# Weight sums of a decoder layer in four steps, each set behind a finished piece of the scan

## The chip, the cores and the metric

The kernel runs on 1 core of one Trainium2 chip. The metric is the device time of one execution in microseconds. The kernel before ran at a median of 1055.19 us over 3 runs (1046.66 to 1056.02). The engines are named as the profile names them: PE (TensorE, matrix products; PEld is its weight load), DVE (VectorE), ACT (ScalarE), POOL (GpSimd) and SP (SyncE, which only issues DMAs here).

## What is computed

One decoder layer in float32 over 16 learned leading tokens and 512 tokens of width 1024, with a token mixer of two branches and an MLP:

```python
u = rmsnorm(h, mix_norm_w[i])
proj = u @ w_in[i]
...
y_pool = pool_mixer(u_pool, pool_w_group[i], pool_scale[i]) @ w_pool_up[i]
y_ssd = mamba2_branch(z, xbc, dt_raw, conv_w[i], conv_b[i], dt_bias[i], a_log[i],
                      d_skip[i], ssd_norm_w[i]) @ w_ssd_out[i]
h = h + (gate_pool * y_pool + gate_ssd * y_ssd) @ w_o[i]

v = rmsnorm(h, mlp_norm_w[i])
hid = jax.nn.relu(v @ w_ff1[i])
h = h + (hid * hid) @ w_ff2[i]
```

The pool mixer subtracts each channel from its causal mean over 2, 4, 8 or 16 tokens and mixes groups of 256 channels. The Mamba-2 branch has 8 groups of 4 heads; each group projects x, B, C and z, runs a short causal convolution over x, B and C, and scans the tokens in chunks of 128 with decays that come from dt.

## The kernel before

Channels lie on the 128 partitions and tokens along the free axis. Every float32 product is made from a high and a low part of each operand (`whi`/`wlo` for weights, `uh`/`ul` for the normed input), three matmuls for one product. Weights arrive from `in_w` in blocks of 128 x 1024 through three `raw` buffers: SP issues the load, ACT rounds the block to `whi` (L94), DVE forms the rest as `wlo` (L96).

Some products are done in pairs with seven half-size products instead of eight (a Strassen-Winograd scheme). They need sums of weight quarters: t1 = b11 + b12, s3 = b12 + b22, t2 = t1 + b22 and t4 = t2 + b21. These are formed in DRAM by accumulating DMAs that POOL issues, one **set** after the other (`weight_sums`, L807). There are 16 sets: 3 for the scan's projections (`fx`, used from group 4 on), 6 for the first MLP matrix (`f1`) and 7 for the second (`f2`, which need t1 and s3 alone). The profile calls their results `fx_t`, `fx_s`, `f_t` and `f_s`. Seven sets are issued in groups 0 to 6, three in the pool stage, six ahead of the MLP.

The stages in order of time are: the projection of group 0 (`group_proj`, L498) with norm and dt; four gates and the normed input (`norm_u`, whose `u_d` goes to DRAM); then for each group g the scan (`ssd`, L558) woven with the projection of group g + 1; then the pool stage (`pool_pair`, L930, and `pool_mix`); the merge with gates; w_o; and the MLP.

- `weave` (L687) takes turns: one piece of the scan, then one piece of the list `fill`. The list is worked through one generator after the other: the next group's projection first, then `sums_of_u` (sums of u halves, loaded back from `u_d`), then `weight_sums_at`.
- `ssd` has seven pieces: decay exponentials; states and mask (L638); two halves of y (L646 to L659); squares and their rounded sum `qh` (L663 to L666); the norm factor; the normed output. It begins with the load of `abc`, the decay rows of the group's heads to all partitions (L566), into a single buffer that the `py` products (L652) of the group before read last. ACT uses it at L597.
- `tc.issue_after(i)` makes an engine issue the instructions of a block behind instruction i of that engine. Apart from this and the data dependences, the order on each engine comes from a planner that simulates the program with modelled times and takes what is ready, earlier program text first. On the chip each engine follows that order strictly. POOL waits in front of a DMA for everything that the DMA needs, so what stands behind it in the queue waits too.
- In the groups a set is placed behind the `abc` load (or the last u load) of the same group, L823 to L830.
- POOL's queue also carries the stores of `acs_d` (L373), `u_d` (L403), gates (`gate_d`, L709) and output parts (`acc_d`, L743 and L774), the loads of u halves (L840), of `acc` and of the gates `m1` for the merge (L1003 and L1005), and `ht` (L1146).
- In `pool_pair` seven products run per pair, A11, A12, S2, S1, S3, S4 and A22. A12 has a one-bank PSUM tile `y`. The others go into two halves of one two-bank tile: `c` (A11, S2, S3, A22) and `z` (S1, S4). L964 to L977 read them between the products.

Of the kernel before, what the change touches and what calls it, by code (L numbers as in the profile page):

```python
# [50 lines left out]
BC_PAIRS = (5, 6)  # L51
PAIRS = [(k, g) for g in range(G) for k in "bx" if g in (BC_PAIRS if k == "b" else X_PAIRS)]

SETS_AT = {0: 1, 1: 1, 2: 1, 3: 1, 4: 1, 5: 1, 6: 1}
SETS_POOL = 3

PLAIN = 4
# [6 lines left out]
def kernel(ctx: ExitStack, tc, xT, x, w, fx, f1, f2, vec, fnw, out):  # L64
# [88 lines left out]
    dec = const.tile([P, 4, HEADS], F32, name="dec")  # L153
    cdec = const.tile([P, 4, HEADS], F32, name="cdec")
    wmeta = const.tile([P, HEADS], F32, name="wmeta")
    dve.memset(wmeta, 0.0)

    u_stack = ExitStack()
# [246 lines left out]
            dve.tensor_tensor(ul[k], xt[k], uh[k].bitcast(F32), op=ALU.subtract)  # L405


    def conv(dst, src, ct):
        n = dst.shape[-1]
        e = src.shape[-1] - n  # L410
        act.activation(dst, src[:, e:], AF.Identity, bias=col(V_CB, ct), scale=col(V_CW, ct * 4 + 3))
        for j in range(1, 4):
            o = max(0, j - e)
            dve.scalar_tensor_tensor(dst[:, o:], src[:, e + o - j : e + n - j],
                                     col(V_CW, ct * 4 + 3 - j), dst[:, o:], op0=ALU.mult, op1=ALU.add)
        act.activation(dst, dst, AF.Silu)

    def group_tiles(g):
        xc = gc.tile([P, 2, L], F32, tag="xc", name=f"xc{g}")
# [78 lines left out]
    def group_proj(g, cur, gate=None):  # L498

        first = g == 0  # L500
        xc, bt, ct, zt = cur

        def plain(dst, t, skip):
            if first and (dst is bt or dst is ct):
                view = viewB if dst is bt else viewC
            else:
                runs, view = wide(psum2(f"px{g}_{t}"), skip)
                proj(runs, block(), X if first else U)
            conv(dst, first_raw(t, view, skip) if first else view, t)
# [36 lines left out]
        if first:  # L546
            dve.tensor_tensor(zt, ps.rearrange("p (i t) -> p i t", i=2),
                              rsb[:, NM:].unsqueeze(1).to_broadcast([P, 2, SEQ]), op=ALU.mult)
            act.activation(zf, zf, AF.Silu)
        else:  # L550
            act.activation(zf, ps, AF.Silu)
        yield
# [5 lines left out]
    def ssd(g, cur):  # L558
# [52 lines left out]

        if g < G - 1:
            done[g] = decay()
        yield

        pc = psum1(f"pcb{g}")
# [19 lines left out]
        for rs_ in ((slice(0, 2), slice(2, R)) if g == G - 1 else (slice(0, R),)):  # L636
            n = rs_.stop - rs_.start
            masked[g] = dve.tensor_tensor(dm[:, rs_], dm[:, rs_], cbm.unsqueeze(1).to_broadcast([P, n, 4, P]),  # L638
                                          op=ALU.mult)
        yield  # L640

        yt = gs.tile([P, 2, SEQ], F32, tag="yt", name=f"yt{g}")
        for i in range(2):
            po = psum1(f"po{g}_{i}")
            for c in range(4):
                pe.matmul(po[:, c * P : (c + 1) * P],  # L646
                          flat(st[c])[:, i * P : (i + 1) * P], ct[:, ctok(c)], start=True, stop=True)
            py = psum1(f"py{g}_{i}")
            for c in range(4):
                for j in range(2):  # L650
                    r = 2 * i + j
                    pe.matmul(py[64 * j : 64 * j + 64, c * P : (c + 1) * P],  # L652
                              xdt[:, c, r, :], dm[:, r, c, :], start=True, stop=True)
            y = yt[:, i, :]
            dve.tensor_tensor(y, po, eb[:, i, :], op=ALU.mult)
            dve.tensor_tensor(y, y, py, op=ALU.add)
            dve.scalar_tensor_tensor(y, xc[:, i, NM:], col(V_DS, 2 * g + i), y,
                                     op0=ALU.mult, op1=ALU.add)
            dve.tensor_tensor(y, y, zt[:, i, :], op=ALU.mult)  # L659
            yield  # L660
# [3 lines left out]
        dve.tensor_tensor(sq[:, 0, :], sq[:, 0, :], sq[:, 1, :], op=ALU.add)  # L664
        qh, ql = col_sums(f"g{g}", sq[:, 0, :], gs, ("qh", "ql"))
        yield  # L666
        pn = psum1(f"png{g}")
        pe.matmul(pn, ones_r, qh, start=True, stop=False)
# [40 lines left out]
            nc.gpsimd.dma_start(gate_d[d], o)  # L709


    cur = group_tiles(0)
# [33 lines left out]
    def out_part():  # L746
# [42 lines left out]
        for d in range(2, NK):  # L789
# [5 lines left out]

    sets = [("fx", n) for n in range(fx.shape[0])] + [
            ("f2", 0), ("f2", 1), ("f1", 0), ("f1", 1), ("f1", 2), ("f2", 2), ("f2", 3), ("f1", 3),
            ("f2", 4), ("f1", 4), ("f2", 5), ("f1", 5), ("f2", 6)]  # L800
    assert len(sets) == fx.shape[0] + f1.shape[0] + f2.shape[0]
    SUMS = {"fx": ("t1", "s3", "t2", "t4"), "f1": ("t1", "s3", "t2", "t4"), "f2": ("t1", "s3")}
    wsum = {(*t, n): dram.tile([P, 1040], F32, name="{}{}_{}".format(*t, n))[:, :1024]
            for t in sets for n in SUMS[t[0]]}
    sums_load = {}

    def weight_sums():  # L807
        t = sets.pop(0)
        src = {"fx": fx, "f1": f1, "f2": f2}[t[0]][t[1]]
        o = {n: wsum[(*t, n)] for n in SUMS[t[0]]}  # L810
        put = nc.gpsimd.dma_start
        put(o["t1"], src[B11])
        put(o["s3"], src[B12])
        put(o["t1"], src[B12], accum_op=ALU.add)
        end = put(o["s3"], src[B22], accum_op=ALU.add)
        if "t2" in o:
            put(o["t2"], o["t1"])
            put(o["t2"], src[B22], accum_op=ALU.add)
            put(o["t4"], o["t2"])
            end = put(o["t4"], src[B21], accum_op=ALU.add)  # L820
        return end

    def weight_sums_at(g):  # L823

        with tc.issue_after(sums_load.get(g, abc_load[g]).ins):
            end = weight_sums()
        for _ in range(SETS_AT[g] - 1):
            with tc.issue_after(end.ins):
                end = weight_sums()
        yield  # L830

    def sums_of_u(ks, g):

        one, two = HF
# [1 line left out]
        def load(k):  # L836
            a, b = raw_pair("u", k)
            with tc.issue_after(abc_load[g].ins):
                for t, kk in ((a, k), (b, k + 4)):
                    sums_load[g] = nc.gpsimd.dma_start(t, u_d[kk])  # L840
            return a, b

        def combine(a, b, behind):
# [86 lines left out]
    def pool_pair(p, behind=None):  # L930
# [92 lines left out]
    for n in range(1, 4):  # L1023
# [765 lines left out]
```

## Time and profile before

| What | us |
| --- | --- |
| runs, median of 3 | 1055.19 (1046.66 to 1056.02) |
| the profiled execution, its own time | 1056.63 |
| its span, first to last instruction | 1054.9 |
| ACT busy | 617.6 |
| DVE busy | 805.7 |
| POOL busy, issue of DMAs among it | 111.0 |

The mean granted clock of PE in that execution was 0.978. A row of the order in time reads: start in us, length in us, engine, line, operation, output<-inputs, shapes, count, and in brackets how long the engine was idle before it and what ended that. A row of the chain that ended last has start, length and what the chain spent that time in. A row of the DMA list has output<-input, issuing queue, count, KB of one, and the median us from issue to landing. SP's and POOL's DMA rows show the issue, not the transfer.

### The profile page before, as it was taken

Reading aid. Unit: us, or ns where it says so; the run is one execution under the profiler, and the core shown is the slowest. Engines: PE = TensorE matmul, PEld = TensorE weight load, DVE = VectorE, ACT = ScalarE, POOL = GpSimd, SP = SyncE. Lnnn points to the kernel's source line nnn. Section 1 sums busy time; section 2 is a strip of 40 time slices with the busy share of each in tenths; the row PEclk is TensorE's granted clock in tenths of the full one; section 3 lists DMA queues with packets and bytes.
Section 4 is the critical chain, followed back from the end, with each engine's and each line's share of the span. In section 5 each row is a group of like instructions: output and inputs, shape, how many; then the busy total and the mean of one; then the engine's idle time right before and its main releaser. Section 6 shows DMA issues by size and latency. Waiting matters only on the chain.

```text
span 1054.9 us, 15609 instructions
## 1 busy us (share of the span) xinstructions
PE 1012.0 (96%) x6023; PEld 886.6 (84%) x6023; DVE 805.7 (76%) x1163; ACT 617.6 (59%) x873; POOL 111.0 (11%) x178
## 2 busy tenths in 40 slices
PE   9999799999899899999998999999999999999997
PEld 7889698988687788988987888888889999999986
DVE  7978588968743667989577765787898788788785
ACT  7666749485925534866433443348755666665654
POOL 0131110121001100101321000121111000000000
PEclk9999899999899799999999999999999999999999
DMA  7376583587256734764878653369898745544532
GB/s 251 99 284 170 175 219 111 186 195 248 65 196 193 206 109 152 168 181 111 225 235 244 185 209 100 136 166 275 263 272 240 223 141 160 180 144 157 159 100 80
DMA packets 62922, 190.28 MB, mean 180 GB/s; under 512 B 7360, under 2 KB 8704, under 8 KB 61824
## 3 DMA queue, kind: packets, MB, share of 16 engines
q1 hardware_dynamic: 40896, 110.58, 31.4%
q0 software_dynamic: 21232, 77.80, 28.9%
q8 instruction: 47, 0.77, 0.3%
q10 hardware_dynamic: 720, 0.91, 0.2%
q14 instruction: 27, 0.22, 0.1%
HBM read 178.90 MB, written 62.78 MB: 229 GB/s over the span
## 4 chain that ended last, share of the span: by engine, by line
PE 72%; issue 7%; DVE 7%; ACT 6%; DMA 6%; POOL 1%; SPq 0%; POOLq 0%; ACTq 0%; DVEq 0%
PE px L1408 8%; PE alpha L1476 6%; PE px L1411 4%; PE px L195 3%; PE alpha L1479 3%; DMA raw<-in_w 3%; PE pgs L195 3%; PE pz L195 2%; PE px L197 2%; DMA abc<-acs_d 2%; PE pqx L475 2%; PE wo_alpha L1170 1%; PE pf L128 1%; PE pf L129 1%; PE pf L131 1%
## 5 line engine op out<-in xcount | busy, mean ns | idle before, releaser
L94 ACT CAST whi<-raw 128x1024 fp32r<-128x1024 f32 (+2 forms) x86 | 85.8, 1009 | 77.1 <-DMA raw<-in_w 19.5
L96 DVE TENSOR_TENSOR wlo<-raw,whi 128x1024 fp32r<-128x1024 f32 (+2 forms) x86 | 99.9, 1168 | 30.4 <-ACT whi L94 22.4
L195 PE MATMUL px<-uh,whi 128*128 128x264 f32 (+1 forms) x256 | 67.2, 299 | 0.0
L197 PE MATMUL px<-ul,whi 128*128 128x264 f32 (+1 forms) x256 | 65.4, 291 | 0.0
L1183 DVE TENSOR_TENSOR ht<-ht,alpha 128x1024 f32<-128x1024 f32 x35 | 42.7, 1219 | 29.1 <-PE alpha L1476 29.1
L1106 ACT CAST shi<-rawf 128x1024 fp32r<-128x1024 f32 x42 | 44.2, 1053 | 28.7 <-PE alpha L1479 18.2
L1476 PE MATMUL alpha<-shi,hh 128*128 128x512 f32 x140 | 55.2, 394 | 0.0
L1479 PE MATMUL alpha<-shi,hl 128*128 128x512 f32 x140 | 54.7, 391 | 0.0
L1107 DVE TENSOR_TENSOR slo<-rawf,shi 128x1024 fp32r<-128x1024 f32 x42 | 51.1, 1218 | 0.6 <-ACT shi L1106 0.6
L195 PEld LDWEIGHTS px<-uh,whi 128*128 128x128 f32 x256 | 50.0, 195 | 1.0 <-issue 0.9
L197 PEld LDWEIGHTS px<-ul,whi 128*128 128x128 f32 x256 | 49.9, 195 | 0.1
L1411 PE MATMUL px<-vsl,shi 128*128 128x256 f32 x192 | 47.4, 280 | 0.0
L1408 PE MATMUL px<-vsh,shi 128*128 128x256 f32 x192 | 47.4, 281 | 0.0
L195 PE MATMUL pz<-uh,whi 128*128 128x512 f32 x112 | 44.5, 397 | 0.0
L197 PE MATMUL pz<-ul,whi 128*128 128x512 f32 x112 | 44.0, 393 | 0.0
L94 ACT CAST whip<-rawp 128x1024 fp32r<-128x1024 f32 (+1 forms) x24 | 22.4, 943 | 31.3 <-PE pqb L478 11.9
L96 DVE TENSOR_TENSOR wlop<-rawp,whip 128x1024 fp32r<-128x1024 f32 (+1 forms) x24 | 26.1, 1087 | 16.3 <-ACT whip L94 12.4
L1476 PE MATMUL alpha<-slo,hh 128*128 128x512 f32 x140 | 37.4, 389 | 0.0
L1408 PEld LDWEIGHTS px<-vsh,shi 128*128 128x128 f32 x192 | 36.2, 188 | 0.9
L1411 PEld LDWEIGHTS px<-vsl,shi 128*128 128x128 f32 x192 | 36.1, 188 | 0.9
L1411 PE MATMUL px<-vl,shi 128*128 128x256 f32 x144 | 36.1, 283 | 0.0
L1408 PE MATMUL px<-vh,shi 128*128 128x256 f32 x144 | 36.0, 282 | 0.0
(626 smaller groups left out, 3192.9 us busy)
## 6 DMA issues: line engine op xcount, KB each, us to landing
raw<-in_w SPq DMA_DIRECT2D x92, 512.0 KB, 4.8
f_t<-in_f POOLq DMA_DIRECT2D x38, 512.0 KB, 6.7
f_s<-in_f POOLq DMA_DIRECT2D x26, 512.0 KB, 8.0
b<-in_f SPq DMA_DIRECT2D x21, 512.0 KB, 4.7
rawf<-in_f SPq DMA_DIRECT2D x36, 256.0 KB, 3.1
rawf<-f_t SPq DMA_DIRECT2D x36, 256.0 KB, 3.2
abc<-acs_d POOLq DMA_DIRECT2D x8, 1024.0 KB, 8.0
fx_t<-in_fx POOLq DMA_DIRECT2D x12, 512.0 KB, 5.9
```

The costliest lines, as they stand in the source:

```text
L94: act.copy(hi[:, c], raw[:, c])
L96: dve.tensor_tensor(lo[:, c], raw[:, c], hi[:, c].bitcast(F32), op=ALU.subtract)
L195: pe.matmul(o, wt, rhs[0][k][:, c], start=part == 0 and k == 0, stop=part == 1 and k == NK - 1)
L197: pe.matmul(o, wt, rhs[1][k][:, c], start=False, stop=False)
L475: pe.matmul(o, wk, f[k][0], start=start and not low and k == 0, stop=stop and low == 1 and k == 3, skip_group_check=True)
L1106: splits.append((act.copy(hi, src), dve.tensor_tensor(lo, src, hi.bitcast(F32), op=ALU.subtract)))
L1107: dve.tensor_tensor(lo, src, hi.bitcast(F32), op=ALU.subtract)))
L1183: added[0] = dve.tensor_tensor(o, o, src, op=op)
L1408: pe.matmul(ps, m, f[k][0], start=start and not low and k == 0, stop=stop and low == 1 and k == 3, skip_group_check=True)
L1411: pe.matmul(ps, m, f[k][1], start=False, stop=False, skip_group_check=True)
L1476: pe.matmul(ps[t], hh[:, p, seg, st], m, start=bool(first and not low and p == 0), stop=bool(last and low and p == 1), skip_group_check=True)
L1479: pe.matmul(ps[t], hl[:, p, seg, st], m, start=False, stop=False, skip_group_check=True)
```

## The change

It moves and regroups the weight sums, and with them two smaller things.

- A set is issued in steps (four for `fx` and `f1`, two for `f2`): first all plain copies from the weights at once (t1, s3, and now also t2 = b22 and t4 = b21), then t1 and s3 with their second terms, then t2 += t1, then t4 += t2. There are eight DMAs to a full set in both kernels.
- Ahead of each step POOL copies one column of a tile, `mark[0]`, to a new tile `seen`, and the step is placed behind that copy. `mark[0]` is set as the program text is laid down: by the convolutions and z of group 0's projection, and by five pieces of `ssd`. In the groups `weight_sums_at` runs at the end of `fill`, when the last mark is `qh` of the group.
- One set is issued during the projection of group 0. Groups 0 to 6 have one each, the pool stage three, and five are left ahead of the MLP.
- In `pool_pair`, `z` becomes a one-bank PSUM tile of its own from the pool of four that `y`, the gates and the mixing products use.
- The seven loads of `m1` move from the start of the pool stage to behind the second `pool_mix`.

```diff
+    def weight_steps():
...
+        put(o["t1"], src[B11])
+        end = put(o["s3"], src[B12])
+        if "t2" in o:
+            put(o["t2"], src[B22])
+            end = put(o["t4"], src[B21])
+        yield end
+        put(o["t1"], src[B12], accum_op=ALU.add)
+        yield put(o["s3"], src[B22], accum_op=ALU.add)
+        if "t2" in o:
+            yield put(o["t2"], o["t1"], accum_op=ALU.add)
+            yield put(o["t4"], o["t2"], accum_op=ALU.add)
...
+    def weight_sums_at():
+        for _ in range(len(SUMS[sets[0][0]])):
+            if not steps:
+                steps.append(weight_steps())
+            at = pool.tensor_copy(seen, mark[0])
+            with tc.issue_after(at.ins):
+                next(steps[0])
+            yield
+        assert next(steps.pop(), None) is None
...
     cur = group_tiles(0)
-    gp0 = group_proj(0, cur)
-    for _ in gp0:
+    early = weight_sums_at()
+    for _ in group_proj(0, cur):
+        next(early, None)
+    for _ in early:
         pass
+    first_part[0] = False
...
-        put(o["t1"], src[B11])
-        put(o["s3"], src[B12])
-        put(o["t1"], src[B12], accum_op=ALU.add)
-        end = put(o["s3"], src[B22], accum_op=ALU.add)
-        if "t2" in o:
-            put(o["t2"], o["t1"])
-            put(o["t2"], src[B22], accum_op=ALU.add)
-            put(o["t4"], o["t2"])
-            end = put(o["t4"], src[B21], accum_op=ALU.add)
-        return end
-
-    def weight_sums_at(g):
-
-        with tc.issue_after(sums_load.get(g, abc_load[g]).ins):
-            end = weight_sums()
...
-        if g in SETS_AT:
-            fill.append(weight_sums_at(g))
+        for _ in range(SETS_AT.get(g, 0)):
+            fill.append(weight_sums_at())
...
-        c = psum2(f"pxx{p}")
-        c, z = c[:, :HALF], c[:, 512 : 512 + HALF]
-        y = psum1(f"py{p}")[:, :HALF]
+        c = psum2(f"pxx{p}")[:, :HALF]
+        y, z = (psum1(f"p{i}{p}")[:, :HALF] for i in "yz")
...
-    for d in range(NK - 1):
-        t_load = nc.gpsimd.dma_start(m1[d], gate_d[d])
...
+        if n == 1:
+            for d in MERGE:
+                with tc.issue_after(mixed[0].ins):
+                    if d < NK - 1:
+                        nc.gpsimd.dma_start(m1[d], gate_d[d])
```

The marks are set at these places: after the convolution's last step in group 0 (`dst[:, :1]`), after z of group 0 (`zf[:, :1]`), and in `ssd` after the decays (`xdt`), the states (`st[3]`), each half of y, and `qh`.

More of the change, by code (lines that the diff above doesn't have):

```diff
@@ L52 @@
 PAIRS = [(k, g) for g in range(G) for k in "bx" if g in (BC_PAIRS if k == "b" else X_PAIRS)]
-SETS_AT = {0: 1, 1: 1, 2: 1, 3: 1, 4: 1, 5: 1, 6: 1}
+SETS_AT = {g: 1 for g in range(7)}
 SETS_POOL = 3
@@ L155 @@
     wmeta = const.tile([P, HEADS], F32, name="wmeta")
+    seen = const.tile([P, 1], F32, name="seen")
     dve.memset(wmeta, 0.0)
@@ L416, in conv @@
         act.activation(dst, dst, AF.Silu)
+        if first_part[0]:
+            mark[0] = dst[:, :1]
     def group_tiles(g):
@@ L709, in gate_pool, with weight_sums @@
             nc.gpsimd.dma_start(gate_d[d], o)
+    sets = [("fx", n) for n in range(fx.shape[0])] + [
+            ("f2", 0), ("f2", 1), ("f1", 0), ("f1", 1), ("f1", 2), ("f2", 2), ("f2", 3), ("f1", 3),
+            ("f2", 4), ("f1", 4), ("f2", 5), ("f1", 5), ("f2", 6)]
+    assert len(sets) == fx.shape[0] + f1.shape[0] + f2.shape[0]
+    SUMS = {"fx": ("t1", "s3", "t2", "t4"), "f1": ("t1", "s3", "t2", "t4"), "f2": ("t1", "s3")}
+    wsum = {(*t, n): dram.tile([P, 1040], F32, name="{}{}_{}".format(*t, n))[:, :1024]
+            for t in sets for n in SUMS[t[0]]}
+    def weight_steps():
+        t = sets.pop(0)
+        src = {"fx": fx, "f1": f1, "f2": f2}[t[0]][t[1]]
+        o = {n: wsum[(*t, n)] for n in SUMS[t[0]]}
+        put = nc.gpsimd.dma_start
+        put(o["t1"], src[B11])
[9 more added lines that the diff above has]
+            yield put(o["t4"], o["t2"], accum_op=ALU.add)
+    def weight_sums():
+        for end in weight_steps():
+            pass
+        return end
+    def weight_sums_at():
[7 more added lines that the diff above has]
+        assert next(steps.pop(), None) is None
+    steps = []
     cur = group_tiles(0)
-    gp0 = group_proj(0, cur)
-    for _ in gp0:
+    early = weight_sums_at()
+    for _ in group_proj(0, cur):
+        next(early, None)
+    for _ in early:
         pass
+    first_part[0] = False
     for d in range(GATES_FIRST):
@@ L793, in out_part @@
             yield
[L798 to L812, printed above, removed]
-        put(o["s3"], src[B12])
-        put(o["t1"], src[B12], accum_op=ALU.add)
-        end = put(o["s3"], src[B22], accum_op=ALU.add)
-        if "t2" in o:
-            put(o["t2"], o["t1"])
-            put(o["t2"], src[B22], accum_op=ALU.add)
-            put(o["t4"], o["t2"])
-            end = put(o["t4"], src[B21], accum_op=ALU.add)
-        return end
-    def weight_sums_at(g):
-        with tc.issue_after(sums_load.get(g, abc_load[g]).ins):
-            end = weight_sums()
[L827 to L830, printed above, removed]
     def sums_of_u(ks, g):
@@ L839, in load @@
                 for t, kk in ((a, k), (b, k + 4)):
-                    sums_load[g] = nc.gpsimd.dma_start(t, u_d[kk])
+                    nc.gpsimd.dma_start(t, u_d[kk])
             return a, b
```

6 lines of the change are left out of this document (added).

## The prediction

> **What bounds the kernel now.** I read the page first, then the busy time by stretches, then the order of time on the engines at the places where TensorE loses time.
>
> ```profile
> PE 1012.0 (96%) x6023; PEld 886.6 (84%) x6023; DVE 805.7 (76%) x1163; ACT 617.6 (59%) x873; POOL 111.0 (11%) x178
> ```
>
> TensorE is busy for 1012.0 of 1054.9 us, so at most 42.9 us of idle time can be won, and what the clock loses behind idle time. No matrix product is added or removed, so the question is only where TensorE stands still. The second view cuts the span into stretches (columns: length, then busy time and instructions of PE, PEld, DVE, ACT, POOL, then the granted clock, the DMA share and GB/s).
>
> ```profile
> 20.00:60.00 40.00, 39.77 (x253) 33.65 (x253) 36.72 (x72) 29.49 (x44) 6.56 (x12) 1.00 0.47 149
> 60.00:100.00 40.00, 39.46 (x295) 36.58 (x294) 29.90 (x49) 22.70 (x32) 8.42 (x14) 1.00 0.77 237
> 100.00:140.00 40.00, 34.05 (x208) 31.18 (x209) 27.16 (x45) 27.31 (x37) 6.60 (x10) 0.87 0.61 163
> 220.00:260.00 40.00, 36.62 (x267) 33.20 (x266) 33.61 (x53) 25.32 (x37) 7.47 (x11) 0.96 0.75 209
> 260.00:300.00 40.00, 34.96 (x159) 28.45 (x159) 27.78 (x42) 30.16 (x40) 2.00 (x3) 0.91 0.43 133
> 300.00:400.00 100.00, 91.01 (x514) 78.50 (x514) 54.35 (x76) 44.57 (x67) 9.99 (x16) 0.91 0.57 165
> 560.00:600.00 40.00, 33.52 (x203) 29.79 (x204) 30.44 (x44) 16.03 (x25) 6.26 (x9) 0.91 0.78 219
> 600.00:1055.00 455.00, 449.19 (x2480) 391.49 (x2478) 359.79 (x466) 258.82 (x370) 27.30 (x41) 1.00 0.58 177
> ```
>
> Idle time is 40 minus PE's busy time, and what the clock costs is the length times one minus the granted clock. That gives 5.95 + 5.2 = 11.1 us in 100 to 140; 3.38 + 1.6 = 5.0 in 220 to 260; 5.04 + 3.6 = 8.6 in 260 to 300; 8.99 + 9.0 = 18.0 in 300 to 400; 6.48 + 3.6 = 10.1 in 560 to 600. From 600 on the clock is full and PE has no room worth the name. So the change can act at a handful of places, and I go through those.
>
> The first is the boundary between group 0 and group 1. POOL's queue there:
>
> ```profile
> 73.97 0.54 POOL L812 DMA_DIRECT2D fx_t<-in_fx  x1
> ...
> 81.60 0.85 POOL L814 DMA_DIRECT2D fx_t<-in_fx  x1 [6.56 <-DMA fx_t<-in_fx]
> ...
> 102.51 0.81 POOL L820 DMA_DIRECT2D fx_t<-in_fx  x1 [3.50 <-DVE rau L846]
> 103.04 0.85 POOL L566 DMA_DIRECT2D abc<-acs_d  x1
> ```
>
> POOL issues in order and stands in front of each DMA until the one it builds on has landed (the idle time in brackets). One set of weight sums holds the queue from 73.97 to 102.51, and the load of group 1's decay rows (abc) comes right behind. Its buffer was free earlier: the sum that reads the last py product of group 0 starts at 98.98. ScalarE then waits for that load, and TensorE for ScalarE and VectorE:
>
> ```profile
> 98.98 0.67 DVE L656 TENSOR_TENSOR yt<-yt,py 128x512 f32<-128x512 f32 x1
> ```
> ```profile
> 113.06 1.28 ACT L597 ACT_TABLE_LOAD   x1 [8.25 <-DMA abc<-acs_d]
> ```
> ```profile
> 117.42 0.40 PE L578 MATMUL ptm<-ident,xc 128*128 128x128 f32 x1 [2.75 <-ACT xc L416]
> 122.08 0.48 PE L586 MATMUL ptx<-ident,xc 128*128 128x128 f32 x1 [3.19 <-DVE xddm L579]
> ```
>
> 2.75 + 3.19 are the 5.94 us of idle time in that stretch.
>
> **Part by part. The pool pairs.** Before, the products into c and z share one PSUM tile; after, z has its own, like y. In the trace a product into one half waits for the read of the other half:
>
> ```profile
> 551.75 0.39 PE L958 MATMUL pxx<-t1h,whiS 128*128 128x264 f32 x1 [0.48 <-ACT pu L968]
> ...
> 575.63 0.59 PE L958 MATMUL pxx<-uh,whiD 128*128 128x264 f32 x1 [3.35 <-DVE pu L974]
> ...
> 597.75 0.39 PE L958 MATMUL pxx<-uh,whiD 128*128 128x264 f32 x1 [0.52 <-DVE pu L974]
> ```
> ```profile
> 569.07 0.43 DVE L972 TENSOR_TENSOR pu<-pu,pxx 128x264 f32<-128x264 f32 x1 [0.51 <-PE pxx L958]
> ...
> 573.82 0.69 DVE L938 TENSOR_TENSOR sm<-raw,raw 128x512 f32<-128x512 f32 x1 [3.73 <-DMA raw<-in_w]
> ...
> 575.16 0.42 DVE L974 TENSOR_TENSOR pu<-pu,pxx 128x264 f32<-128x264 f32 x1
> ```
>
> At 575.63 the last product (A22) goes into c. The only read of c that it must follow is L972, at 569.07. It waits for L974, which reads z, and L974 stands on VectorE behind L938, which waits for a weight load. Six waits of about 0.5 us, from the first of 0.48 to the last of 0.52, make 3.0; this one makes 3.35; the clock in 560 to 600 lost 3.6. All three gone is 9.95. I take 8.5, since the mixing product behind A22 needs VectorE work that also stands behind L938. The low end is the 3.0 alone. A loss is possible too: y, z, a gate and two mixing products now share four one-bank slots, and a z that waited for a slot in each of three pairs would cost 3 x 0.5 = 1.5. I see no such wait, because each of those tiles is read soon after its product.
>
> **Weight sums out of group 0's scan.** One set moves into the projection of group 0, so 16 sets lie as 1 early, 7 in the groups, 3 in the pool stage and 5 in the tail, where it was 0, 7, 3 and 6. A group's set now follows a one-column copy on POOL of qh, the squared sums of the scan. The marks of earlier pieces are overwritten by the time the generator runs, so all steps of a group stand behind that one piece. The next abc load can go when py is read, and qh is computed from what py gives, so abc is ready first; in group 2, for one, by 8.4 us:
>
> ```profile
> 200.39 0.55 POOL L566 DMA_DIRECT2D abc<-acs_d  x1 [26.93 <-PE py L652]
> ```
> ```profile
> 208.81 0.62 ACT L307 CAST qhg<-sqg 128x512 fp32r<-128x512 f32 x1 [1.08 <-DVE sqg L664]
> ```
>
> So abc(1) should go at about 99 instead of 103.04. Landing times and what they are compared with:
>
> ```profile
> abc<-acs_d POOLq DMA_DIRECT2D x8, 1024.0 KB, 8.0
> raw<-in_w SPq DMA_DIRECT2D x92, 512.0 KB, 4.8
> f_t<-in_f POOLq DMA_DIRECT2D x38, 512.0 KB, 6.7
> f_t<-f_t POOLq DMA_DIRECT2D x12, 512.0 KB, 4.5
> ```
> ```profile
> 103.04 9.96 DMA abc<-acs_d
> 254.22 6.98 DMA raw<-in_w
> 326.47 7.21 DMA abc<-acs_d
> 564.65 9.07 DMA raw<-in_w
> ```
>
> At the median of 8.0 abc(1) is there at 107 instead of 113.0, six us earlier, against 5.94 us of idle time. I take 9 of the 11.1; the ends are 0 (the gap is ScalarE's own work) and 11.1.
>
> **The later boundaries.** In 220 to 300 the sums before run into weight loads: 6.98 us against a median of 4.8, on the chain that ended last. With that set moved behind qh this load comes 2.2 us earlier. Of the 13.6 us lost there I take 4 (ends 0 and 13.6). In 300 to 400 the sums move from just behind abc(5) to a few us later. That load took 7.21, already under its median of 8.0, so I take 1 of 18.0; the rest there belongs to the pairs' own convolutions.
>
> **What it costs.** Early set: the DMA share in 20 to 60 is 0.47, and with a set beside it, in 60 to 100, it was 0.77 and PE lost 0.54 us. On POOL the early steps stand ahead of acs_d, the u_d and gate stores and abc(0):
>
> ```profile
> 38.10 0.65 ACT L416 ACTIVATE bt<-bt 128x528 f32<-128x528 f32 x1
> ...
> 47.13 0.65 ACT L416 ACTIVATE xc<-xc 128x528 f32<-128x528 f32 x1 [1.05 <-DVE xc L414]
> ```
> ```profile
> 46.60 2.00 POOL L373 DMA_DIRECT2D acs_d<-dacs  x4 [12.16 <-DVE dacs L370]
> 67.31 0.55 POOL L566 DMA_DIRECT2D abc<-acs_d  x1
> ```
>
> From bt at 38.75 the last step can be issued after landings of 6.7 + 6.7 + 4.5, at about 57, ahead of 67.31. I take 1; the ends are 0 and 11.1, the price of the late abc at the next boundary. **Bursts:** four copies now start at once where two did, and right at the boundaries; at 0 to 1, 1 to 2 and 6 to 7 no set started just there before. A weight load beside sums took 9.07 instead of 4.8, 4.3 more; with a clock loss like the 3.6 of 560 to 600, three such come to 3 x 7.9 = 23.7 at worst, and to nothing where the load is prefetched. I take 6, near the 0.54 row, since most loads have slack. The 28 copies on POOL have no like in the trace but the 128x1 fills of 0.10 us:
>
> ```profile
> 0.31 0.10 POOL L1781 MEMSET const-float32-0.0<- 128x1 f32 x1 [0.31 <-issue]
> ```
>
> 28 x 0.10 = 2.8 at most if each held somebody up; I take 0, as POOL waits most of the time. The Trainium skill speaks against this copy: "GPSIMD Engine Reference", Key points, says that this engine shares its SBUF interfaces with VectorE and that they contend. By that rule the sum would be up to 2.8 us higher, and no row here shows such a slowdown. The gate loads (m1) move behind the second mix and are due only in the merge, past 600, where PE is full: 0. The number of DMAs and the bytes stay the same; the dependent chain of a set gets shorter, six DMAs to four.
>
> **Sum:** 1056.63 (profiled execution: span 1054.9 and 1.7 around it) - 8.5 - 9 - 4 - 1 + 1 + 6 = 1041.1. The median of the runs shown is 1.44 lower than that execution, so I forecast 1040.
>
> A rule on the clock: a gap of 2.33 us sits at 341.60 in a stretch whose clock was 0.91, so here gaps well under 3 us came with a lost clock.
>
> ```profile
> 341.60 0.39 PE L475 MATMUL pqb<-uh,whip 128*128 128x264 f32 x1 [2.33 <-ACT rab L480]
> 285.91 0.80 PE L128 MATMUL pso<-yh,whi 128*128 128x512 f32 x1 [3.42 <-ACT whi L94]
> ```
>
> "TensorE: Matmul & The Clock Gate" of the Trainium skill (the section on the HAM clock gate) puts the clock at half after an idle window of about 3.4 us. By that, the 3.42 us gap at 285.91 would only have to shrink a little to give back all 3.6 us of its stretch, and the sum would be about 1037.5; by the row at 341.60 it would not, and I count the clock only where the gap goes.
>
> **The rivals.** *Given back:* the bursts behind qh hit the weight loads at the boundaries. For it: the 9.07 us load. Against it: 60 to 100. With 16 to 20 us of cost it ends at 1051 to 1055; I say 1053. *Inherent gap:* abc(1) comes early but the boundary stays ScalarE's, and only the PSUM tile pays: 1055.19 - 8.5 + 2 (the early set and one burst) = 1049. *More:* the idle time of 220 to 300 goes in large part too (9 more of 13.6) and the bursts cost little: 1040 - 9 - 5 = 1026. *Slower:* the order on POOL is set by modelled times; if it puts the sum steps ahead of the next abc load, abc waits for qh and three landings, 6.7 + 6.7 + 4.5 = 17.9 us. A lateness of 4 us cost 11.1 at 0 to 1, so it decides from about 4 us on, and 17.9 us late cost 11.1 + 13.9 = 25. At one later boundary, with the 11.1 at 0 to 1 kept, that is 1056.6 - 8.5 - 4 - 1 + 1 + 25 = 1069; with 13.9 more at 0 to 1, 1083; I say 1076. Against it speaks that py precedes qh.
>
> **How the numbers follow.** About 1% (10.6 us) is what a measurement tells from no change: below 1044.6 is faster, above 1065.7 slower. Forecast (1030 to 1047) 0.48, of which 0.43 is below 1044.6; more 0.14; given back 0.18, of which 0.02 above 1065.7; inherent 0.07; slower 0.13. Faster 0.43 + 0.14 = 0.57; slower 0.13 + 0.02 = 0.15; within 0.28. The range 1022 to 1060 leaves out the slower rival and 0.05 at its ends.
>
> **What would show it.** No PE gap behind L974 or L968 in the pool stage and a clock near 1.0 in it; the abc load of group 1 issued near 99 with no chain of sums ahead; no PE gaps of 2.75 and 3.19 us behind it. It is wrong if abc loads stand behind sum steps, if ScalarE's wait for abc grows at any group, or if weight loads beside the bursts take 9 us and PE waits for them.

## The result, and the profile after

| | before | after |
| --- | --- | --- |
| median us | 1050.82 of 8 runs (1046.66 to 1056.02) | 1042.54 of 8 runs (1039.26 to 1046.14) |
| the profiled execution | 1056.63 | 1046.09 |
| its span | 1054.9 | 1044.4 |

The ratio is 0.9918, with a 95% interval of 0.989 to 0.9946: 8.6 us less of 1050.82, a gain just under 1%. The ratios here and below leave out slow executions and need not be the quotients of the medians shown (here 0.9921, 8.3 us). The busy times of the page:

```profile
PE 1011.9 (97%) x6023; PEld 880.8 (84%) x6023; DVE 805.4 (77%) x1163; ACT 617.4 (59%) x873; POOL 128.4 (12%) x206
```

PE does the same work. The span is 10.5 us shorter and PE's idle time in it falls from 42.9 to 32.5, so the profiled gain is idle time. The stretches of the kernel after (columns as in the prediction):

```profile
60.00:100.00 40.00, 35.35 (x227) 32.04 (x227) 23.95 (x40) 21.45 (x31) 7.33 (x13) 0.91 0.52 180
100.00:140.00 40.00, 40.00 (x297) 37.04 (x296) 35.42 (x58) 30.69 (x41) 9.01 (x15) 1.00 0.74 200
...
220.00:260.00 40.00, 39.81 (x294) 36.58 (x293) 34.82 (x57) 29.31 (x41) 5.00 (x8) 1.00 0.47 147
260.00:300.00 40.00, 35.79 (x157) 28.78 (x156) 23.74 (x33) 23.79 (x33) 1.66 (x3) 0.91 0.48 139
300.00:400.00 100.00, 90.30 (x529) 77.04 (x529) 59.20 (x86) 47.71 (x72) 9.90 (x18) 0.93 0.50 151
...
530.00:560.00 30.00, 26.33 (x170) 24.44 (x169) 20.43 (x29) 12.09 (x18) 8.51 (x13) 0.94 1.03 293
560.00:600.00 40.00, 40.00 (x232) 35.25 (x232) 33.50 (x48) 20.51 (x31) 1.45 (x2) 1.00 0.53 169
```

Idle time and lost clock, worked out as in the prediction (length less PE's busy time, and length times one minus the clock), fell at three places and grew at two. In 100 to 140 us 11.1 became 0, in 220 to 300 13.6 became 8.0, in 560 to 600 10.1 became 0. But 60 to 100 went from 0.5 to 4.65 + 3.6 = 8.2, and 530 to 560 from 1.4 to 3.67 + 1.8 = 5.5. The sum over such stretches is no span: it fell by 17.6 us and the span by 10.5, because PE's busy time hardly moved while the mean granted clock rose from 0.978 to 0.985. So the stretches say where time was lost, and the ratios of the runs say how much.

**Where 8 us appeared: 60 to 100.** POOL's queue in order of time:

```profile
53.89 0.84 POOL L744 DMA_DIRECT2D fx_t<-fx_t  x1 [2.25 <-ACT uh L405]
...
62.66 0.86 POOL L745 DMA_DIRECT2D fx_t<-fx_t  x1 [6.68 <-DMA fx_t<-fx_t]
63.23 0.87 POOL L719 DMA_DIRECT2D gate_d<-gp  x1
...
71.72 0.55 POOL L719 DMA_DIRECT2D gate_d<-gp  x1 [4.44 <-ACT gp L717]
72.25 0.55 POOL L572 DMA_DIRECT2D abc<-acs_d  x1
...
104.81 0.55 POOL L572 DMA_DIRECT2D abc<-acs_d  x1 [26.24 <-PE py L660]
112.68 0.64 POOL L756 COPY seen<-qhg 128x1 f32<-128x1 f32 x1 [7.33 <-ACT qhg L308]
```

The last step of the early set stands 6.68 us for the step before it, and the first gate's store goes out only behind it, at 63.23. In the kernel before it went at 55.41:

```profile
55.41 0.54 POOL L709 DMA_DIRECT2D gate_d<-gp  x1 [2.14 <-ACT gp L707]
```

DVE needs the tile that this store empties, ACT needs the abc load that stands on POOL behind the store of DVE's next gate, and PE waits for what ACT makes; one row from each of the three engines' order in time:

```profile
69.93 0.69 DVE L716 TENSOR_TENSOR gp<-pgp,rsb 128x512 f32<-128x512 f32 x1 [4.91 <-DMA gate_d<-gp]
```
```profile
82.17 1.28 ACT L603 ACT_TABLE_LOAD   x1 [5.05 <-DMA abc<-acs_d]
```
```profile
90.96 0.80 PE L654 MATMUL po<-ct,st 128*128 128x128 f32 x2 [4.01 <-ACT st L636]
```

abc(0) was issued at 67.31 before and at 72.25 here, and ACT's wait for it was shorter before:

```profile
75.87 1.28 ACT L597 ACT_TABLE_LOAD   x1 [3.34 <-DMA abc<-acs_d]
```

The rest of POOL's rows show what the change was expected to do: abc(1) waits for the product `py` alone, with no sums ahead of it, and the set comes 8 us behind it, after the copy of `qhg`.

**Where 4 us appeared: 530 to 560.** The pieces of the chain that ended last (start, length, what), and PE's gaps:

```profile
538.49 8.38 DMA raw<-in_w
...
548.33 0.68 DVE wloB L115
```
```profile
549.07 0.75 PE L978 MATMUL pz<-t1h,wloB 128*128 128x264 f32 x4 [2.61 <-DVE wloB L115]
550.88 0.39 PE L978 MATMUL pxx<-uh,whiD 128*128 128x264 f32 x1 [1.06 <-DVE pu L992]
```

A weight load took 8.38 us where their median is 4.6, and the work of VectorE that PE needs stands behind it. The DMA share of the stretch is 1.03: POOL starts the four copies of a set at 536.07 to 537.63, just ahead of that load. The waits behind L974 and L968 of the kernel before are gone.

### The profile page after: what moved, and what is told of

It is laid out like the page before. It is cut to its first block, busy times and chain, and to the rows that moved or that the text cites. A ratio compares the mean times of both kernels' runs of the same rounds, so it can differ in the third digit from the quotient of the medians.

```text
span 1044.4 us, 15640 instructions
## 1 busy us (share of the span) xinstructions
PE 1011.9 (97%) x6023; PEld 880.8 (84%) x6023; DVE 805.4 (77%) x1163; ACT 617.4 (59%) x873; POOL 128.4 (12%) x206
## 4 chain that ended last, share of the span: by engine, by line
PE 75%; DMA 8%; ACT 7%; DVE 5%; issue 4%; POOL 0%; SPq 0%; DVEq 0%; ACTq 0%; POOLq 0%
PE px L1431 8%; PE alpha L1499 6%; PE px L196 5%; PE px L1434 4%; PE alpha L1502 3%; PE pgs L196 3%; PE pz L196 3%; PE px L198 2%; DMA raw<-in_w 2%; PE pqx L480 2%; DMA abc<-acs_d 2%; PE po L654 1%; PE py L660 1%; PE wo_alpha L1193 1%; PE pf L129 1%
## 5 line engine op out<-in xcount | busy, mean ns | idle before, releaser
L96 DVE TENSOR_TENSOR wlop<-rawp,whip 128x1024 fp32r<-128x1024 f32 (+1 forms) x24 | 26.1, 1086 | 15.6 <-ACT whip L94 9.5
```

Of the source, the lines that this page charges most:

```text
L96: dve.tensor_tensor(lo[:, c], raw[:, c], hi[:, c].bitcast(F32), op=ALU.subtract)
```

## The experiments

All times are medians of all runs. In the three groups of runs the kernel before gave 1049.18, 1050.47 and 1047.21, so ratios compare better than microseconds. The lost time by stretch, worked out as above from one profile each:

| | ratio (interval) | median | 60-100 | 100-140 | 140-220 | 220-300 | 300-400 | 400-530 | 530-600 |
| --- | --- | --- | --- | --- | --- | --- | --- | --- | --- |
| before | 1 | 1050.82 | 0.5 | 11.1 | 1.6 | 13.6 | 18.0 | 1.8 | 11.5 |
| after | 0.9918 (0.989 to 0.9946) | 1042.54 | 8.2 | 0 | 0 | 8.0 | 16.7 | 2.1 | 5.5 |
| e1 no early set | 0.985 (0.981 to 0.9891) | 1033.13 | 0 | 0 | 0 | 6.4 | 12.3 | 1.0 | 2.0 |
| e2 early set split | 0.9905 (0.9869 to 0.994) | 1037.97 | 0.5 | 0 | 0 | 6.0 | 17.8 | 1.0 | 5.3 |
| e3 z tile alone | 0.9917 (0.9881 to 0.9954) | 1039.92 | 0.9 | 5.8 | 0 | 10.9 | 16.0 | 1.7 | 1.6 |
| e4 no set in group 0 | 0.9928 (0.99 to 0.9957) | 1040.28 | 0.2 | 0 | 1.0 | 16.8 | 12.7 | 2.3 | 7.8 |
| e5 z tile undone | 1.0 (0.997 to 1.0029) | 1051.73 | 7.6 | 0 | 0 | 4.4 | 11.2 | 0.8 | 17.7 |
| e6 sets ahead of abc | 0.9899 (0.9849 to 0.9948) | 1040.26 | 0.1 | 0 | 0 | 7.7 | 15.6 | 1.0 | 3.0 |
| e7 fewer in the pool stage | 0.983 (0.9774 to 0.9885) | 1031.59 | 0.1 | 0 | 0 | 6.4 | 12.3 | 0.5 | 2.3 |
| e8 old chain | 0.985 (0.9811 to 0.9889) | 1034.91 | 0 | 0 | 0 | 7.0 | 12.8 | 2.0 | 2.3 |
| e9 right behind abc | 0.9958 (0.9928 to 0.9988) | 1043.69 | 0.5 | 0 | 4.2 | 10.3 | 12.0 | 7.9 | 1.7 |
| e10 no set in group 4 | 0.9841 (0.9779 to 0.9903) | 1032.71 | 0.2 | 0 | 0 | 5.3 | 12.1 | 1.2 | 1.4 |

On PE, DVE, ACT and SP the kernels with z in its own tile, e3 among them, issue the same instructions in the same order as the kernel after; e4 and e5, without it, have the order of the kernel before. The two orders differ in the pool stage alone, which the planner lays out anew when z has its own tile. So all but the z tile, with the order that comes with it, is POOL's queue. (What the expectations call the abc store is the load of `abc`.)

**e1: no early set.**

```diff
-    early = weight_sums_at()
     for _ in group_proj(0, cur):
-        next(early, None)
-    for _ in early:
         pass
```

> The changed kernel without the early set: no set of sums in group 0's projection, one in each of groups 0 to 6, three in the pool stage, six ahead of the MLP. The order on PE, DVE, ACT and SP stays that of the changed kernel; only POOL's queue differs. Theory (queue): the early steps hold POOL's queue, so that the first gate store and abc(0) go late; without them PE loses at most 1 us in 60 to 100 (8.2 now: 4.65 idle and 3.6 of clock), abc(0) is issued near 67 and the kernel is 6 to 8 us faster than the changed one, about 1035. Rival (room made later): the early set takes sums away from the later stages, and without it what was won in 60 to 100 is lost again in 400 to 600: within 3 us of the changed kernel, 1040 to 1045.

Stretches, and POOL in order of time:

```profile
60.00:100.00 40.00, 40.00 (x299) 37.07 (x298) 30.57 (x50) 22.93 (x32) 4.32 (x8) 1.00 0.50 173
...
530.00:560.00 30.00, 28.01 (x193) 25.49 (x191) 26.47 (x41) 14.02 (x23) 5.60 (x8) 1.00 0.84 251
```
```profile
96.68 0.54 POOL L572 DMA_DIRECT2D abc<-acs_d  x1 [22.50 <-PE py L660]
...
535.49 0.86 POOL L735 DMA_DIRECT2D f_t<-in_f  x1
536.01 0.86 POOL L736 DMA_DIRECT2D f_s<-in_f  x1
```

The stall is gone, and 0.9918 less 0.985, some 7 us, is the price of the early set, as the theory had it. In 530 to 560 it is cheaper too: without the early set every later place in the list of sets holds the set before it, and where the kernel after starts four copies at 536 this one starts two at 535.49.

**e2: the early set split**, its last step placed behind the load of abc(0).

```diff
+    for n, _ in enumerate(group_proj(0, cur)):
+        if n < 3:
+            next(early, None)
...
+        if g == 0:
+            with tc.issue_after(abc_load[g].ins):
+                next(steps[0])
```

> The changed kernel with only the last of the four early steps (t4 += t2) moved behind the load abc(0) on POOL; same DMAs, same bytes, the first three steps at their old places. Theory (queue): what cost 8.2 us in 60 to 100 was POOL standing 6.7 us in front of that step with the gate store and abc(0) behind it; then abc(0) is issued at 66 to 68 instead of 72, the idle time of 4.0 us at 91 is gone, and the kernel is 6 to 8 us faster than the changed one, about 1035. Rival (DMA load): the bytes of the early set slow the weight loads and stores in 40 to 70; then the loss in 60 to 100 stays above 5 us and the time within 2 us of the changed kernel.

60 to 100 loses 0.5 instead of 8.2, which shows that the one waiting step made the stall. The time did not follow: by the ratios only 1.4 us are won of the theory's 6 to 8, with an interval that overlaps those of e1 and of the kernel after, and beside e1 it is 4.8 us slower by the medians of the same group of runs. In the profiles 530 to 600 still loses 5.3, against 2.0 in e1, and 300 to 400 loses 17.8, against 12.3, nearly all of that difference as clock. How the early set's 7 us divide between the waiting step and the rest is therefore open.

**e3: the z tile alone**, in the kernel before.

```diff
-        c = psum2(f"pxx{p}")
-        c, z = c[:, :HALF], c[:, 512 : 512 + HALF]
-        y = psum1(f"py{p}")[:, :HALF]
+        c = psum2(f"pxx{p}")[:, :HALF]
+        y, z = (psum1(f"p{i}{p}")[:, :HALF] for i in "yz")
```

> The kernel before with one thing changed: z in a one-bank PSUM tile of its own in the pool pairs. POOL's order is that of the kernel before. Theory (shared tile): the seven waits of a product for a read of the other half vanish, and with them most of the 11.5 us that PE lost in 530 to 600 (idle 7.9, clock 3.6); 7 to 9 us faster than before, about 1043. Rival (late load): the wait only moves to the next product, since VectorE stands before a late weight load all the same, as in the changed kernel, where 530 to 560 lost 5.5 us; then 2 to 6 us faster. No gain at all would say that the later stage was not bound by PE.

```profile
100.00:140.00 40.00, 35.78 (x240) 32.83 (x239) 30.49 (x52) 29.43 (x39) 6.86 (x11) 0.96 0.68 178
...
560.00:600.00 40.00, 38.42 (x210) 32.81 (x209) 31.18 (x44) 20.03 (x31) 4.39 (x6) 1.00 0.79 234
```

The pool stage loses 1.6 instead of 11.5 and the ratio is that of the whole change. A gap at the first boundary stays, with 5.8 us lost there; the kernel before, with the same order on POOL, lost 11.1.

**e4: no set in group 0**, in the kernel before; groups 1 to 6 each take the set that the group before them had, and one more is left ahead of the MLP.

```diff
-SETS_AT = {0: 1, 1: 1, 2: 1, 3: 1, 4: 1, 5: 1, 6: 1}
+SETS_AT = {1: 1, 2: 1, 3: 1, 4: 1, 5: 1, 6: 1}
```

> The kernel before without the set of sums in group 0's scan: groups 1 to 6 have one set each, the pool stage three, seven are left ahead of the MLP. The order on PE, DVE, ACT and SP is that of the kernel before, so only POOL's queue and the DMA traffic differ. Theory (late abc): abc(1) is issued near 99 instead of 103.0 and lands by 106; PE loses at most 1.5 us in 100 to 140 instead of 11.1, and the kernel is 9 to 11 us faster than before, about 1041. Rival (ScalarE's own work): the boundary from group 0 to 1 is bound by ScalarE's order whenever abc comes; then at least 5 us stay lost there and the kernel is at most 4 us faster.

```profile
100.00:140.00 40.00, 40.00 (x296) 37.04 (x296) 35.39 (x58) 31.91 (x42) 6.52 (x10) 1.00 0.64 179
...
220.00:260.00 40.00, 35.47 (x232) 30.79 (x233) 33.00 (x55) 27.41 (x39) 7.40 (x11) 0.91 0.86 245
```
```profile
222.59 1.50 PE L618 MATMUL pcb<-ct,bt 128*128 128x128 f32 x8 [3.03 <-DVE xddm L579]
```

With no sums ahead of abc(1) the boundary from group 0 to group 1 costs nothing: the gaps of 2.75 and 3.19 us were the late abc. The time, 7.5 us less by the ratio, is short of the theory's 9 to 11. A gap of 3.03 us stands at a later boundary instead. There abc is not late; the load of a u half (`rbu`), which POOL issues between steps of the sets, is, and DVE stands still until it has landed, at 214.49 in the trace (the row's own view names no releaser, "issue"):

```profile
214.56 0.43 DVE L845 TENSOR_TENSOR rbu<-rau,rbu 128x264 f32<-128x264 f32 x1 [11.17 <-issue]
```

**e5: the z tile undone** in the kernel after, so that the order on POOL stands alone.

```diff
-        c = psum2(f"pxx{p}")[:, :HALF]
-        y, z = (psum1(f"p{i}{p}")[:, :HALF] for i in "yz")
+        c = psum2(f"pxx{p}")
+        c, z = c[:, :HALF], c[:, 512 : 512 + HALF]
+        y = psum1(f"py{p}")[:, :HALF]
```

> The kernel after, with the z product and the copies of its sum back in the tiles that they shared before; the order of the weight sums on POOL's queue stays that of the kernel after. Theory (two parts that add, each in its own stretch): the order on POOL is worth the stretches 100-140 and 220-300 us and costs the stretch 60-100, the z tile is worth the stretch 530-600. So 60-100 shows about 8 us of idle time and lost clock as in the kernel after, 100-140 about 0, and 530-600 has 8 to 11 us as in the kernel before instead of 5.4: 1044 to 1050 us. Rival (the z tile is the whole gain): the time of the kernel before, 1049 us or above, and 100-140 has its 11 us back.

```profile
60.00:100.00 40.00, 36.02 (x235) 32.76 (x234) 24.14 (x40) 21.28 (x30) 7.32 (x13) 0.91 0.53 179
...
530.00:560.00 30.00, 24.34 (x158) 22.44 (x157) 18.25 (x27) 11.08 (x19) 6.76 (x11) 0.89 0.98 266
560.00:600.00 40.00, 34.90 (x184) 29.89 (x183) 26.38 (x38) 16.28 (x26) 0.00 (x0) 0.91 0.33 110
```
```profile
564.96 0.59 PE L979 MATMUL pxx<-uh,whiD 128*128 128x264 f32 x1 [3.11 <-DVE pu L995]
```

Each stretch does what the theory of two parts says, but the time is the rival's: no gain at all. 100 to 140 is won and 60 to 100 lost, and the pool stage loses 17.7 where the theory had 8 to 11: the shared tile (3.11 behind the read of z, which stands on VectorE behind a weight load of 8.78 us) and late weight loads add up. In the whole change, then, the order on POOL bought nothing and the z tile bought everything, with the early set eating what the rest of the order gave.

**e6 and e8: place against form.** Both go from e1, and both have a set in each of groups 0 to 6. e6 puts the sets where the kernel before has them, ahead of the next abc load, in the new form of four steps and without the `seen` copies. e8 keeps the new places and gives the sets the old form, six steps that depend on each other.

```diff
     # e6
+    def weight_sums_at(g):
+        with tc.issue_after(sums_load.get(g, abc_load[g]).ins):
+            weight_sums()
+        yield
...
     # e8
-            put(o["t2"], src[B22])
-            end = put(o["t4"], src[B21])
...
-            yield put(o["t2"], o["t1"], accum_op=ALU.add)
-            yield put(o["t4"], o["t2"], accum_op=ALU.add)
+            put(o["t2"], o["t1"])
+            yield put(o["t2"], src[B22], accum_op=ALU.add)
+            put(o["t4"], o["t2"])
+            yield put(o["t4"], src[B21], accum_op=ALU.add)
```

> The kernel after without its early set and without the copies of pieces already seen; the sums of groups 1 to 6 are four steps with the independent first copies, but they stand on POOL's queue where the kernel before has them, ahead of the next group's abc store. Against the kernel after without its early set (1033 us) only the place on the queue differs. Theory (place): the abc store waits behind the set's steps again, so the stretch 100-140 loses about 11 us and 220-260 about 5: 1040 to 1050 us. Rival (form): a set of four waits instead of six is short enough at any place, and the abc store goes out some 4 to 5 us earlier than in the kernel before: 100-140 below 3 us, 1033 to 1037 us.

> The kernel after without its early set, its steps of groups 1 to 6 at the same places behind finished pieces, but each set in the form of the kernel before: two first copies that the later adds depend on, six steps in a row instead of four. Theory (place): where a set stands behind the abc store and the set is spread over the group, two more steps cost POOL's queue a few us that nobody waits for: within 4 us of the kernel without the early set, 1031 to 1037 us, 100-140 below 2 us. Rival (form): the chain of six is still at work when the next group's stores are due, 100-140 and 220-260 lose 5 us or more: 1040 to 1048 us.

e3, e6, e8 and e1 make a square. At the old place the time is 1039.92 with the old form and 1040.26 with the new one; at the new place 1034.91 and 1033.13; the ratios are 0.9917 and 0.9899, and 0.985 twice. The form is worth nothing that can be measured, the place 5 to 7 us, although for the new form alone (e6 against e1) the intervals overlap. (e3 also has the `m1` loads at their old place; no run takes that apart.) The theories of e6 and e8 are right in time, but the one of e6 had the loss in 100 to 140, and there it is 0. POOL and two stretches of e6:

```profile
95.51 0.81 POOL L745 DMA_DIRECT2D fx_t<-fx_t  x1 [4.97 <-DVE wlo L96]
97.47 0.58 POOL L572 DMA_DIRECT2D abc<-acs_d  x1 [1.15 <-PE py L660]
```
```profile
220.00:260.00 40.00, 37.19 (x251) 32.69 (x251) 33.74 (x54) 28.53 (x38) 5.54 (x8) 1.00 0.72 202
...
300.00:400.00 100.00, 89.41 (x546) 77.33 (x545) 62.44 (x90) 49.18 (x74) 10.80 (x18) 0.95 0.53 160
```

The last step of the four-step set is issued just before `py` is read, so the form alone does mend the first boundary, as the rival says. The loss against e1 is spread: 2.2 us more in 220 to 260 and 3.3 more in 300 to 400, most of the latter as clock. For 220 to 260 the trace names a wait: DVE stands 6.69 us for the load of `rbu`, 3.97 in e1. The rest was not settled.

**e7: fewer sums in the pool stage**, `SETS_POOL = 2` in e1.

> The kernel after without its early set, and with one quad's set fewer among the pool stage's work and one more ahead of the MLP. Theory (a burst of copies slows the loads that the pool stage waits for): the stretch 530-560, which lost 2.0 us without the early set and 5.4 in the kernel after, comes to below 1, and the time is 0 to 2 us below that of the kernel without the early set: 1031 to 1034 us. Rival (the sums ahead of the MLP are late for its loads): 600 to the end loses 3 us or more beyond its 6.4 to 7.3, 1035 to 1040 us.

The time is in the theory's range but its stretch isn't: 530 to 560 loses 2.3, not under 1. Its interval covers e1's ratio, so nothing is shown.

**e9: the set right behind the abc load**, in e1, with no `seen` copies and so no wait for `qh`.

```diff
-            at = pool.tensor_copy(seen, mark[0])
-            with tc.issue_after(at.ins):
-                next(steps[0])
+        with tc.issue_after(abc_load[g].ins):
+            weight_sums()
...
-SETS_AT = {g: 1 for g in range(7)}
+SETS_AT = {g + 1: 1 for g in range(7)}
```

> The kernel after without its early set and without the copies of pieces already seen; the four-step sets stand on POOL's queue right behind the abc store of the next group (groups 1 to 7), with no wait for the squared sums in front of a step, so the first four copies start with the abc load and the chain runs without a pause. Theory (what counts is that a set stands behind the abc load and not in front of it): within 3 us of the kernel after without its early set, 1030 to 1036 us, 100-140 and 220-260 together below 3 us. Rival (the copies must be held back and spread behind the finished piece, since they slow the abc load itself and the weight loads of the boundary): abc lands 2 us or more later than the 7.3 us of the kernel without the early set, 1038 to 1044 us.

The time is the rival's, and some 10 us of gain are gone. POOL, the chain that ended last, ACT and PE at the boundary from group 1 to group 2:

```profile
140.74 0.57 POOL L572 DMA_DIRECT2D abc<-acs_d  x1 [16.57 <-PE py L660]
141.29 0.54 POOL L735 DMA_DIRECT2D fx_t<-in_fx  x1
```
```profile
144.76 8.07 DMA raw<-in_w
```
```profile
152.91 1.04 ACT L94 CAST whi<-raw 128x1024 fp32r<-128x1024 f32 x1 [4.67 <-DMA raw<-in_w]
153.86 0.61 ACT L308 CAST qhg<-sqg 128x512 fp32r<-128x512 f32 x1
```
```profile
154.52 0.65 PE L678 MATMUL png<-qhg,ones_r 128*128 128x512 f32 x1 [2.62 <-ACT qhg L308]
```

The copies start with the abc load, and the weight load of 144.76 takes 8.07 us beside them. ACT stands 4.67 us for it, `qh` stands behind it on ACT, and PE waits for `qh`. The abc loads were not slower, as the rival had it (their median is 6.8, against 7.3 in e1); the weight loads were the victims, here and in 400 to 530, where 7.9 us were lost. (Some u loads stand behind the steps in e9 and come a few us later, too; what that adds was not separated.) The small copy that waits for `qh` is therefore no ornament: it holds the four copies back until the weight load that stands ahead of `qh` on ACT has landed.

**e10: no set in group 4**, `if g != 4` in e1's `SETS_AT`; the later places take the set before theirs, and one more is left ahead of the MLP.

> The kernel after without its early set and without the set of group 4 (the one at 313 to 330 us), which goes to the sums ahead of the MLP. Theory (what is left in 260-300 and 300-400 is the work of the pairs of groups 5 and 6 and not the sums): those two stretches keep 16 to 18 us together, 1030 to 1036 us. Rival (the sums there still slow the loads of the pairs): they fall below 13 us, 1026 to 1030 us.

260 to 400 keeps 16.4 us, as the theory says, and the time lies in its range. What is left there up to 396, where the next set begins, comes with no sums beside it.

## Why the prediction was right in its time, and what in it was wrong

The time forecast was 1040 and it came to 1042.54. That it is so near is in part luck: the sum had a gain of 15.5 us, and 8.6 were measured. Its start, three runs with a median of 1055.19, was 4.4 above the median of eight, and one term, the early set, was wrong by 6; from the median of eight the same sum would have given 1035.3. The ratio of 0.9918 lies in the case "within 1%", which had 0.28, not in "faster", which had 0.57.

- **Pool pairs, 8.5 us.** Right in size. The z tile alone gave 0.9917, 8.7 us, and taking it out of the kernel after cost the same 0.8%. No PE gap stands behind L974 or L968 any more. The working did not see that the planner also changes the order of this stage. In the kernel before, L974 (575.16) stands on VectorE behind L938 of the next pair (573.82), which waits for a weight load; in the kernel after, the read of z (now L994) stands ahead of that sum (now L959):

```profile
562.92 0.43 DVE L994 TENSOR_TENSOR pu<-pu,pz 128x264 f32<-128x264 f32 x1
...
568.50 0.68 DVE L959 TENSOR_TENSOR sm<-raw,raw 128x512 f32<-128x512 f32 x1
```

  e3 and e5 change the tile and this order together, so no run shows what the tile alone would give in the old order.
- **Boundary 0 to 1, 9 of 11.1.** Right in its cause: e4, which takes the sums from in front of abc(1) and does nothing else there, leaves 0 and is 7.5 us faster. The rival "inherent gap" falls with it. In the trace all of it went; how much that is in time is less sure, as e3 lost only 5.8 there with the old order on POOL.
- **220 to 300, 4 of 13.6; 300 to 400, 1 of 18.0.** The profile of after has 5.6 and 1.3 less, but in 220 to 300 not for the reason given. The prediction blamed the weight load of 254.22; no PE gap over 0.3 us stands between 243.66 and 280.50 in the kernel before, and 260 to 300 still loses 7.8 of 8.6. What went is 220 to 260, from 5.0 to 0.2, where VectorE stood for the load of `rbu`, issued between steps of the sets; before and after:

```profile
221.27 0.43 DVE L845 TENSOR_TENSOR rbu<-rau,rbu 128x264 f32<-128x264 f32 x1 [7.39 <-issue]
```
```profile
213.24 0.43 DVE L866 TENSOR_TENSOR rbu<-rau,rbu 128x264 f32<-128x264 f32 x1 [2.85 <-DMA rbu<-u_d]
```

  In the kernel before that load landed at 221.19, and in e4, where this wait is longest (11.17), the gap of PE behind it is the largest too (3.03); no run moves this load alone. The statement that the rest of 300 to 400 belongs to the pairs' own convolutions fits e10.
- **Bursts, +6.** Right as a mechanism, wrong as to place. Behind `qh` no loss shows at the first two boundaries between groups (0 in 100 to 220); e9, which starts them with the abc load, shows the late weight load and the price, some 10 us. In the kernel after they hit once, in the pool stage at 538.49, where 530 to 560 loses 5.5. That this is near the 6 of the term is luck.
- **The order on POOL without the early set**, that is 9 + 4 + 1 - 6 = 8 us of gain, measured 0.9917 less 0.985, 7 us.
- **The early set, +1 us, ends 0 and 11.1.** This is the term of the sum that failed; it measured 7 us. The step said that "the last step can be issued after landings of 6.7 + 6.7 + 4.5, at about 57, ahead of 67.31", and asked only whether abc(0) would be late. The step came at 62.66, as its landings took longer: from the third step at 53.89 to this one 8.8 us went by, where 4.5 were assumed. The first victim was not abc. It was the gate store right behind it in the queue, whose tile VectorE was to fill again; the chain from there made abc(0) 4.9 us late. In the kernel before that store goes at 55.41, so even a step at 57 would have stood in its way. The text named "the u_d and gate stores" as standing behind the steps and did not follow who waits for them. Taking out that one step (e2) removes the stall of 8.2 us but gives back only 1.4 us by the ratios; the rest of the 7 us was not pinned down.
- **The copies on POOL, 0.** Right in the sum; the bound of 2.8 us was no bound, since a copy took far longer than the fills it was priced by:

```profile
L756 POOL COPY seen<-qhg 128x1 f32<-128x1 f32 x24 | 15.4, 641 | 48.0 <-ACT qhg L308 47.8
```

  24 of them were busy for 15.4 us, 641 ns each, and no engine is seen to wait for one. "GPSIMD Engine Reference" of the Trainium skill, Key points, says that this engine shares its SBUF interfaces with VectorE and contends with VectorE instructions that run in a two-port mode or have two SBUF inputs. Here VectorE was busy for 805.7 us before and 805.4 after, so no run shows it.
- **Slower: abc behind the sum steps.** At the boundaries between groups it did not happen; `py` precedes `qh` in every group. Two of the signs of being wrong did come at group 0, by way of the early set: abc(0) stood behind its steps, and ScalarE's wait for abc(0) grew from 3.34 to 5.05 us.

## What to carry to other kernels

When a chain of dependent DMAs moves to an earlier place on an in-order queue, follow each transfer that it now stands in front of to the engine that needs its landing or its freed buffer, not only the one load that was late before. Put such a chain behind the load that the next stage needs, and let its first copies wait for something that is finished after that stage's weight loads. The version to keep is e1: all of the change but the early set, 0.985 of the time before; e7, e8 and e10 cannot be told from it.

## What the runs showed of the hardware

PE's lost clock does not follow from the length of a gap alone. PE and stretches in e1, then in the kernel before, at the same matmul:

```profile
365.51 0.44 PE L584 MATMUL ptm<-ident,xc 128*128 128x128 f32 x2 [2.63 <-ACT xc L419]
```
```profile
360.00:380.00 20.00, 17.37 (x130) 15.50 (x128) 16.39 (x25) 7.85 (x14) 0.00 (x0) 1.00 0.38 120
```
```profile
386.76 0.44 PE L578 MATMUL ptm<-ident,xc 128*128 128x128 f32 x2 [2.62 <-ACT xc L416]
```
```profile
381.00:401.00 20.00, 17.38 (x116) 15.79 (x115) 16.12 (x23) 6.83 (x13) 0.00 (x0) 0.91 0.39 120
```

Behind a gap of 2.63 us the clock stayed full; behind one of 2.62 us its mean over 20 us was 0.91. "TensorE: Matmul & The Clock Gate" of the Trainium skill, in its part on the HAM clock gate, says that the window over which activity is judged runs free of the kernel, which fits the scatter; its idle window of about 3.4 us as the condition does not fit, as the gap of 2.62 us was shorter. Over the 24 executions of the kernel before that ran beside e1 to e4 the mean clock varies from 0.979 (1057.85 us, the longest) to 0.993; the shortest, 1038.84 us, had 0.992. So the clock's part of a forecast (3.6 us here and there) is drawn anew in each execution, and may be part of why the kernel before spreads over 9 us in the eight runs of the result.

The stores of the normed input slowed beside the early set, though they are no larger; without it, in e1, they took 2.8 us again, and with its first three steps, in e2, 6.8. DMA rows of the kernel before and of the kernel after:

```profile
u_d<-xt POOLq DMA_DIRECT2D x8, 264.0 KB, 2.8
```
```profile
u_d<-xt POOLq DMA_DIRECT2D x8, 264.0 KB, 8.2
```
